# A streaming-encoder trunk on one Trainium2 core: the down projection's passes begin and end with plain quads, the PSUM banks swap roles, and the last half has three mixed groups

## The chip, the core and the metric

The kernel runs on one NeuronCore of a Trainium2 chip. The core has five engines that run side by side, each with a queue of its own: TensorE (PE) does matrix products into PSUM, VectorE (DVE), ScalarE (ACT) and GpSimd (POOL) do element work, and SyncE (SP) issues most transfers. The time is the device time of one launch in microseconds (us), the median of several runs.

## The reference

The input is `x`, 256 tokens of width 2048 in float32. Two layers follow, and each has a token mixer (a convolution module in layer 0, latent attention in layer 1) and then a squared-ReLU MLP:

```python
def sq_relu_mlp(h, w1, w2):
    return jnp.square(jax.nn.relu(h @ w1)) @ w2

for layer in range(DEPTH):                       # DEPTH = 2
    h = rms_norm(x, norm_mixer_g[layer])
    x = x + (conv_module if layer % 2 == 0 else mla)(h, ...)
    h = rms_norm(x, norm_mlp_g[layer])
    x = x + sq_relu_mlp(h, mlp_w1[layer], mlp_w2[layer])
return rms_norm(x, final_norm_g)
```

`w1` is 2048x8192 and `w2` is 8192x2048. The change lies in the product with `w2`, the down projection.

## The kernel before

**Precision.** Every float32 operand is split in two parts that TensorE takes at full speed: `hi` is a rounded copy (made on ACT, lines 169 and 487) and `lo` is the rest (raw minus `hi`, made on DVE, lines 173 and 488). `mm3` (lines 200 to 204) forms one product as three matmuls: hi*hi, lo*hi and hi*lo. The parts of the weights lie in two rings of `WB = 6` tiles, and the raw weights in a ring of three tiles that SP fills from HBM, 1 MB each. So the weights can be prepared only as far ahead as these rings are free.

**An MLP in halves.** `mlp(layer, ...)` goes through the 8192 hidden columns in two halves (`hf`). In each half the up projection computes eight groups `g` of 512 hidden columns (lines 619 to 660). Each group takes four of the eight PSUM banks in turn, and is then squared, scaled, split and kept in SBUF as `gs[g]`. Then the down projection (lines 661 to 707) multiplies these eight groups with 4096 rows of `w2`. I write a half as (layer, hf), from (0,0) to (1,1).

**Passes and quads.** The down projection goes over the 2048 output columns in two passes of 1024 (`n` = 0 and `n` = 2). One step is a *quad*: 256 rows of `w2` by 1024 columns, for all 256 tokens.
- A *plain* quad (`Sums.plain`, line 548) makes the four output blocks (2 halves of the tokens by 2 column blocks) straight, with 8 products, which are 24 matmuls. Each block adds up in a bank of its own, the four *e* banks.
- A *mixed* quad (`Sums.mixed`, line 535) uses a seven-product scheme in the manner of Strassen and Winograd: 7 products, 21 matmuls. It needs sums and differences of the weight blocks (`mixed_weights`, lines 480 to 500: three subtractions and four lower parts on DVE, against two lower parts for a plain quad) and of the activations (`mixed_inputs`). Three products go to the e banks, four to the *u* banks.

`MIXED` says which groups are mixed in each half: groups 0, 2, 4 and 6 in three halves, and 0, 2 and 4 in (0,1). Each group gives two quads.

**The end of a pass.** When the last mixed quad is done, `Sums.join` (line 565) turns the four u banks into the missing parts of the four blocks: a copy on ACT and four additions on DVE, into four SBUF tiles *a, b, c, d* (`room()`, a ring of four). POOL sends each tile to the residual stream `xs` with an accumulating transfer of 256 KB (`put`, line 563), in the order a, c, d, b. I call these the puts. When the last plain quad is done, `Sums.close` (line 577) adds two e banks to `xs` on DVE (line 583) and sends the other two with a copy on ACT (line 586) and two more puts.

**The order of a pass.** Lines 672 to 684 spread the mixed quads among the plain ones. Before, a pass begins with mixed quads, as many as line 677 gives for the first plain quad (two where four groups are mixed, one where three are); the last mixed quad stands ahead of the third last plain quad (`TAIL = 3`), and `join` ahead of the last but one. `Sums.__init__` (line 524) takes eight banks, the first four as u and the last four as e, in every pass.

**The second pass of a second half.** For `last` halves the pass `n = 2` is done by `product_A` (line 404) with the plain groups, one column block after the other, and the hook `between` (line 691) puts the mixed quads among those of the first block. Its index `u` is -1 ahead of the first plain group. In (1,1) it is followed at once by the final norm: `before` (line 1829) multiplies finished parts of `xs` with the final gain on DVE (`gained`, line 1787), the squares for the norm are made on ACT (line 400), and line 377 adds an e bank to `xs`.

**What sets the order.** The tile framework orders the instructions of each engine when the kernel is built; on the chip each engine goes through its own list in that order, and waits at an instruction until its semaphores are there.

Of the kernel before, what the change touches and what calls it, by code (L numbers as in the profile page):

```python
# [21 lines left out]
T = 2  # L22
# [18 lines left out]
PAD_O = 56  # L41
WB = 6
LOOK = WB // 2 - 1
MIXED = {(0, 0): (0, 2, 4, 6), (0, 1): (0, 2, 4), (1, 0): (0, 2, 4, 6), (1, 1): (0, 2, 4, 6)}
N_MIXED = 4
TAIL = 3


SIDE = {KC - 3: 2, KC - 2: 4}
# [29 lines left out]
def trunk_kernel(  # L79
# [59 lines left out]
    def nm(s):  # L139
        uid[0] += 1  # L140
        return f"{s}_{uid[0]}"


    def acc_tile():
        return psum["acc"].tile([P, NB], F32, tag="acc", name=nm("acc"))
# [45 lines left out]
    def load_split(srcs, nj):  # L191
        return split(load(srcs, nj), nc.vector)

    def rows(w, k0, nk, c0, n):

        return w[k0 * P : (k0 + nk) * P, c0 : c0 + n].rearrange(
            "(j p) n -> p j n", p=P
        )
# [106 lines left out]
    at, cols = 0, []  # L305
# [31 lines left out]
    def step(n=1000):  # L337
        while steps and n > 0:
            n -= 1
            steps.pop(0)()  # L340
# [180 lines left out]
    class Sums:  # L521


        def __init__(self, n):
            self.n = n
            self.u = [acc_tile() for _ in range(4)]
            self.e = [[acc_tile() for _ in range(2)] for _ in range(T)]
            self.begun = set()

        def first(self, ps):  # L530
# [58 lines left out]
    def mlp(layer, ssq, next_gain, finish=None, before=None, beside=None, after_up=None):  # L589

        with ExitStack() as cx:
# [7 lines left out]
            def v_tile():  # L599
                return mp.tile([P, 2, S], F32, tag="v", name=nm("v"), bufs=4)  # L600
# [4 lines left out]
            def scales():  # L605
                r = rms_rstd(ssq[:, :, :NNB], NNB, D, "n")
                r2 = small.tile([P, T], F32, tag="r2", name=nm("r2"))
                nc.vector.tensor_tensor(r2, r, r, op=ALU.mult)
                o = acc_tile()
                for t in range(T):  # L610
                    nc.tensor.transpose(o[:, t * P : (t + 1) * P], r2[:, t : t + 1].broadcast_to([P, P]), ident)
                nc.scalar.activation(r2_row, o[:, :S], AF.Copy)

            for hf in range(HALVES):
                last = hf == HALVES - 1
                mixed = MIXED[layer, hf]
                plain = [g for g in range(ng) if g not in mixed]
                gs = {}
                for g in range(ng):
                    ps = [acc_tile() for _ in range(4)]  # L620
                    c0 = (hf * nkh + 4 * g) * P
                    for u in range(KC // 4):
                        if u == KC // 4 - 1:
                            step()
                        wj = load_split([rows(mlp_w1[layer], 4 * u, 4, c0, NB)], 4)
                        for j in range(4):
                            k = 4 * u + j
                            wh, wl = wj(j)
                            for b in range(4):
                                bs = slice(b * P, (b + 1) * P)  # L630

                                nc.tensor.matmul(ps[b], wh[:, bs], xhl(k), start=k == 0, stop=False)  # L632
                                nc.tensor.matmul(ps[b][:, :S], wl[:, bs], xh(k), start=False, stop=k == KC - 1)  # L633
                        step(6)
                    if hf == g == 0:
                        scales()
                    if beside is not None and g == 2:
                        beside(mp)
                        beside = None
                    if g in mixed or g in plain[len(plain) + len(mixed) - N_MIXED :]:  # L640
                        shape = [P, 2, 7, P] if g in mixed else [P, 4, S]
                        gs[g] = [mp.tile(shape, F32R, tag=f"s{c}", name=nm(f"s{c}"), bufs=N_MIXED) for c in "hl"]
                    else:
                        gs[g] = [mp.tile([P, 4, S], F32R, tag=f"g{c}", name=nm(f"g{c}"), bufs=ng - N_MIXED) for c in "hl"]
                    gh, gl = gs[g]
                    for b2 in range(2):
                        v = v_tile()
                        for b in range(2):
                            o = ps[2 * b2 + b]
                            nc.scalar.activation(v[:, b, :], o[:, S:], AF.Copy)  # L650
                            nc.vector.tensor_tensor(v[:, b, :], o[:, :S], v[:, b, :], op=ALU.add)
                        nc.vector.scalar_tensor_tensor(out=v, in0=v, scalar=0.0, in1=v, op0=ALU.max, op1=ALU.mult)
                        row = r2_row.rearrange("p (a n) -> p a n", a=1).broadcast_to([P, 2, S])
                        nc.vector.tensor_tensor(v, v, row, op=ALU.mult)
                        if g in mixed:
                            mixed_inputs(v, gh[:, b2], gl[:, b2])
                            continue
                        bs = slice(2 * b2, 2 * b2 + 2)
                        nc.scalar.activation(gh[:, bs, :], v, AF.Copy)
                        nc.vector.tensor_tensor(gl[:, bs, :], v, gh[:, bs, :].bitcast(F32), op=ALU.subtract)  # L660
                nssq, add, prepare = residual_stage(last, next_gain)
                w, k_lo = mlp_w2[layer], hf * nkh
                at_kt = lambda i: lambda k, t: gs[k // 4][i][:, k % 4, t * P : (t + 1) * P]
                hi, lo = at_kt(0), at_kt(1)
                ms = [(g, b) for g in mixed for b in range(2)]
                due = []

                def mixed_quad(sums, i):
                    g, b = ms[i]
                    sums.mixed(w, k_lo + 4 * g + 2 * b, gs[g][0][:, b], gs[g][1][:, b], i == len(ms) - 1)  # L670

                for n in range(0, NNB - 2 * last, 2):
                    sums = Sums(n)
                    ks = [4 * g + 2 * b for g in plain for b in range(2)]
                    at = 0
                    for i, k in enumerate(ks):
                        upto = -(-len(ms) * (i + 1) // (len(ks) - TAIL + 1))
                        while at < min(upto, len(ms)):
                            mixed_quad(sums, at)
                            at += 1  # L680
                        if i == len(ks) - 2:
                            sums.join(room)
                        sums.plain(w, k_lo + k, hi, lo, k, i == len(ks) - 1)
                    sums.close(room)
                    if last:
                        due += [n, n + 1]
                if last:
                    sums = Sums(NNB - 2)
                    n2 = NNB - 2

                    def between(n, u, due):
                        if n == n2 and u < len(plain) - 1:
                            lo_i, hi_i = (len(ms) * i // len(plain) for i in (u + 1, u + 2))
                            for i in range(lo_i, hi_i):
                                mixed_quad(sums, i)
                        if n == n2 and u == len(plain) - 1:
                            sums.join(room)

                    if after_up is not None:
                        after_up()  # L700
                    product_A(
                        w, k_lo, nkh, hi, lo, add, prepare, range(n2, NNB), due,
                        finish=(lambda t: finish(nssq, t)) if finish is not None else None,
                        before=lambda: before(nssq),
                        groups=plain, banks={n2 + c: [sums.e[t][c] for t in range(T)] for c in range(2)},
                        begun=sums.begun, beside=between,
                    )
# [3 lines left out]
    with ExitStack() as cx:  # L711
# [235 lines left out]
        with tc.manual_schedule():  # L947
# [149 lines left out]
            for c in range(1, KC + 1):  # L1097
                n = UC * c
# [121 lines left out]
            for m in range(NP):  # L1220
# [25 lines left out]
                for q in {NP - 3: (0, 1, 4), NP - 2: (5, 2, 3), NP - 1: (6, 7)}.get(m, ()):  # L1246
                    t, i = divmod(q, NNB)
# [13 lines left out]
    def rotary_tables(pool):  # L1261
# [54 lines left out]
        nc.scalar.activation(cos, an2, AF.Sin)  # L1316

    ssq = mlp(0, ssq, g_mix[1], beside=rotary_tables)
    repool("a", acc=6, tr=2)


    with ExitStack() as cx:
        at = cx.enter_context(tc.tile_pool(name="at", bufs=1, reuse_waits="tile"))
# [320 lines left out]
        with tc.manual_schedule():  # L1644
# [8 lines left out]
            ps = [[acc_tile() for _ in range(2)] for _ in range(T)]  # L1653
            for k in range(KC):
                u, j = divmod(k, 2)
# [14 lines left out]
            ps = [acc_tile() for _ in range(T)]  # L1670
            for k in range(KC):
                u, j = divmod(k, 4)
# [59 lines left out]
            for g in range(NG):  # L1732
                for i in range(HG):
                    h = g * HG + i

                    n = -(-len(work) // (HG - i))
# [129 lines left out]
```

## Time and profile before

| what | value |
|---|---|
| median of 3 runs | 1953.53 us (1952.42 to 1954.0) |
| profiled execution | 1954.63 us, span 1952.8 us |
| PE, DVE, ACT, POOL busy | 1926.6, 1574.7, 1090.9, 259.2 us |
| mean granted clock of TensorE | 0.998 |

The page gives the busy time of each engine, and groups of instructions by line. `L488 DVE TENSOR_TENSOR lo<-raw,hi` is the DVE instruction of line 488 that writes `lo` from `raw` and `hi`; `x240` is the number of them. The idle time of a group is that of its engine just ahead of these instructions, and the name behind the arrow is what ended most of it. In a table by windows each engine has its busy time in that stretch and, in brackets, the number of its instructions there. A matmul's duration in the trace overlaps with the next one's, so a matmul's price is taken from the length of a stretch without waits, divided by the number of matmuls in it.

The eight down passes stand at 478 to 643 us (0,0), 821 to 990 us (0,1), 1427 to 1592 us (1,0) and 1769 to 1945 us (1,1).

### The profile page before, as it was taken

How to read it: one execution, taken by the hardware profiler on the slowest of the kernel's cores; microseconds unless marked ns; L12 is line 12 of the kernel's file. 1: busy time of each engine (PE TensorE's matmuls, PEld its weight loads, DVE VectorE, ACT ScalarE, POOL GpSimd, SP SyncE). 2: the span in 40 equal slices, each digit the busy share in tenths (PEclk: the TensorE clock that was granted, in tenths of full speed). 3: DMA queues.
4: the chain of work that ended last, by engine and by line, in shares of the span. 5: the costliest groups of instructions: out<-in, count | busy, mean ns of one | idle time of the engine just before them, and what ended most of it. 6: DMA issues, size and time to landing. Idle time of an engine off the chain costs nothing.

```text
span 1952.8 us, 28589 instructions
## 1 busy us (share of the span) xinstructions
PE 1926.6 (99%) x10811; PEld 1683.5 (86%) x10811; DVE 1574.7 (81%) x2436; ACT 1090.9 (56%) x1628; POOL 259.2 (13%) x216
## 2 busy tenths in 40 slices
PE   8999999999999999999999999999999999999997
PEld 8999888888888888888899998888888888888876
DVE  7999988877999677788866665877799967779996
ACT  5667755554555455455556655555555645555554
POOL 6999100000010000001002210000000010000000
PEclk9999999999999999999999999999999999999999
DMA  7765556654686766557764445566547686655755
GB/s 231 209 192 176 168 180 213 193 186 140 217 245 225 238 186 187 168 200 242 218 196 139 129 151 176 190 196 193 177 169 236 206 269 194 186 182 194 233 180 157
DMA packets 222057, 379.15 MB, mean 194 GB/s; under 512 B 16216, under 2 KB 91232, under 8 KB 221664
## 3 DMA queue, kind: packets, MB, share of 16 engines
q1 hardware_dynamic: 214256, 363.28, 58.0%
q0 software_dynamic: 6336, 11.54, 3.3%
q10 hardware_dynamic: 1328, 2.52, 0.4%
q8 instruction: 84, 1.38, 0.3%
q14 instruction: 53, 0.43, 0.1%
HBM read 363.68 MB, written 2.10 MB: 187 GB/s over the span
## 4 chain that ended last, share of the span: by engine, by line
PE 66%; issue 25%; DVE 4%; DMA 3%; ACT 1%; POOL 1%; SPq 0%; DVEq 0%; ACTq 0%; POOLq 0%
PE acc L632 18%; PE acc L633 9%; PE acc L202 9%; PE acc L204 9%; PE acc L203 8%; PE acc L776 8%; PE acc L1239 2%; DMA xs<-v 2%; DVE sum L863 1%; DVE lo L173 1%; POOL xs L563 1%; DVE lo L488 0%; DMA xs<-in_x 0%; ACT hi L169 0%; PE acc L1623 0%
## 5 line engine op out<-in xcount | busy, mean ns | idle before, releaser
L173 DVE TENSOR_TENSOR lo<-raw,hi 128x1024 fp32r<-128x1024 f32 (+2 forms) x511 | 607.7, 1204 | 262.1 <-ACT hi L169 256.7
L169 ACT ACTIVATE hi<-raw 128x1024 fp32r<-128x1024 f32 (+2 forms) x576 | 587.5, 1039 | 371.8 <-PE acc L632 208.5
L632 PE MATMUL acc<-xt,hi 128*128 128x512 f32 x2048 | 710.5, 390 | 0.0
L633 PE MATMUL acc<-xt,lo 128*128 128x256 f32 x2048 | 577.5, 282 | 0.0
L632 PEld LDWEIGHTS acc<-xt,hi 128*128 128x128 f32 x2048 | 384.3, 188 | 80.6
L633 PEld LDWEIGHTS acc<-xt,lo 128*128 128x128 f32 x2048 | 387.1, 189 | 0.2
L487 ACT ACTIVATE hi<-raw 128x1024 fp32r<-128x1024 f32 x240 | 222.5, 948 | 221.7 <-DVE raw L495 123.6
L488 DVE TENSOR_TENSOR lo<-raw,hi 128x1024 fp32r<-128x1024 f32 x240 | 256.1, 1087 | 33.3 <-ACT hi L487 29.3
L563 POOL DMA_DIRECT2D xs<-v x44 | 38.6, 942 | 1502.8 <-DVE lo L173 693.4
L202 PE MATMUL acc<-hi,sh 128*128 128x512 f32 x516 | 202.3, 392 | 5.6 <-ACT hi L487 5.4
L204 PE MATMUL acc<-lo,gh 128*128 128x512 f32 (+1 forms) x516 | 199.7, 388 | 3.2 <-DVE lo L173 3.2
L204 PE MATMUL acc<-lo,sh 128*128 128x512 f32 x516 | 199.5, 390 | 1.7 <-DVE lo L488 1.6
L202 PE MATMUL acc<-hi,gh 128*128 128x512 f32 (+1 forms) x516 | 200.3, 388 | 0.0
L203 PE MATMUL acc<-hi,gl 128*128 128x512 f32 (+1 forms) x516 | 200.0, 388 | 0.0
L776 PE MATMUL acc<-xt,hi 128*128 128x256 f32 x1024 | 180.2, 281 | 0.3 <-ACT b L1058 0.2
L203 PE MATMUL acc<-hi,sl 128*128 128x512 f32 x452 | 176.0, 389 | 0.0
L863 DVE SCALAR_TENSOR_TENSOR sum<-ub,w_dw,sum 128x256 f32<-128x256 f32 x409 | 164.3, 482 | 3.6 <-ACT sum L833 3.0
L173 POOL TENSOR_TENSOR lo<-raw,hi 128x1024 fp32r<-128x1024 f32 x65 | 154.9, 2406 | 17.3 <-ACT hi L169 17.3
L776 PEld LDWEIGHTS acc<-xt,hi 128*128 128x128 f32 x1024 | 154.7, 188 | 1.1 <-ACT xt L1042 0.6
L776 PE MATMUL acc<-xt,lo 128*128 128x256 f32 x512 | 139.2, 279 | 0.0
L202 PEld LDWEIGHTS acc<-hi,sh 128*128 128x128 f32 x516 | 96.9, 188 | 30.2 <-ACT hi L487 10.7
L204 PEld LDWEIGHTS acc<-lo,gh 128*128 128x128 f32 x516 | 96.9, 188 | 23.8 <-DVE lo L173 4.1
(306 smaller groups left out, 2543.6 us busy)
## 6 DMA issues: line engine op xcount, KB each, us to landing
raw<-in_mlp_w SPq DMA_DIRECT2D x256, 1024.0 KB, 5.4
raw<-in_conv_w_pw SPq DMA_DIRECT2D x62, 512.0 KB, 5.1
raw<-in_conv_w_pw SPq DMA_DIRECT2D x16, 1024.0 KB, 5.0
raw<-in_mla_w_o SPq DMA_DIRECT2D x16, 1024.0 KB, 5.4
xs<-v POOLq DMA_DIRECT2D x44, 256.0 KB, 7.2
raw<-in_mla_w_kv_up SPq DMA_DIRECT2D x8, 1024.0 KB, 5.4
raw<-in_mla_w_in SPq DMA_DIRECT2D x8, 576.0 KB, 3.8
raw<-in_mla_w_in SPq DMA_DIRECT2D x4, 1024.0 KB
```

Source lines behind the costliest of these rows:

```text
L169: nc.scalar.activation(hi, raw[:, js, :], AF.Copy)
L173: eng.tensor_tensor(lo, raw, hi.bitcast(F32), op=ALU.subtract)
L202: nc.tensor.matmul(ps, sh, mh, start=start, stop=False)
L203: nc.tensor.matmul(ps, sl, mh, start=False, stop=False)
L204: nc.tensor.matmul(ps, sh, ml, start=False, stop=stop)
L487: nc.scalar.activation(hi, src, AF.Copy)
L488: nc.vector.tensor_tensor(lo, src, hi.bitcast(F32), op=ALU.subtract)
L563: nc.gpsimd.dma_start(self.place(t, c), o, accum_op=ALU.add)
L632: nc.tensor.matmul(ps[b], wh[:, bs], xhl(k), start=k == 0, stop=False)
L633: nc.tensor.matmul(ps[b][:, :S], wl[:, bs], xh(k), start=False, stop=k == KC - 1)
L776: nc.tensor.matmul(pss[c][b][:, :S], w[i][:, bs], (xh, xl)[j](k), start=k == i + j == 0, stop=end and k == k0 + nk - 1 and (i, j) == terms ...
L863: nc.vector.scalar_tensor_tensor(out=out, in0=ubs[c][:, w : w + S], scalar=tap(c, w), in1=base, op0=ALU.mult, op1=ALU.add)
```

## The change

- `MIXED[1, 1]` loses group 6: the last half has three mixed groups, and five plain ones.
- Ahead of the first mixed quad of a pass there are now `HEAD` plain quads, two in the pass `n = 0` and one in the pass `n = 2`. `TAIL` goes from 3 to 2: the last mixed quad stands ahead of the last but one plain quad where four groups are mixed, and `join` directly ahead of the last one. (Where three groups are mixed, line 677's rounding up puts the last mixed quad ahead of the third last plain quad.)
- In the pass `n = 2` of a second half, no mixed quad stands ahead of the first plain group; they are spread over the gaps behind the plain groups.
- The banks: in the pass `n = 0` the first four of the eight banks are now the e banks, and the last four the u banks; in the pass `n = 2` it is the other way round. So the e banks of the second pass are the u banks of the first.

```diff
-MIXED = {(0, 0): (0, 2, 4, 6), (0, 1): (0, 2, 4), (1, 0): (0, 2, 4, 6), (1, 1): (0, 2, 4, 6)}
+MIXED = {(0, 0): (0, 2, 4, 6), (0, 1): (0, 2, 4), (1, 0): (0, 2, 4, 6), (1, 1): (0, 2, 4)}
-TAIL = 3
+HEAD, TAIL = (2, 1), 2
...
             self.n = n
-            self.u = [acc_tile() for _ in range(4)]
-            self.e = [[acc_tile() for _ in range(2)] for _ in range(T)]
+            ps = [acc_tile() for _ in range(8)]
+            e, self.u = (ps[:4], ps[4:])[:: 1 if n == 0 else -1]
+            self.e = [e[2 * t : 2 * t + 2] for t in range(T)]
...
-                    at = 0
+                    at, head = 0, HEAD[n // 2]
                     for i, k in enumerate(ks):
-                        upto = -(-len(ms) * (i + 1) // (len(ks) - TAIL + 1))
+                        upto = -(-len(ms) * (i - head + 1) // (len(ks) - head - TAIL + 1))
                         while at < min(upto, len(ms)):
                             mixed_quad(sums, at)
                             at += 1
-                        if i == len(ks) - 2:
+                        if i == len(ks) - TAIL + 1:
                             sums.join(room)
                         sums.plain(w, k_lo + k, hi, lo, k, i == len(ks) - 1)
...
                         if n == n2 and u < len(plain) - 1:
-                            lo_i, hi_i = (len(ms) * i // len(plain) for i in (u + 1, u + 2))
-                            for i in range(lo_i, hi_i):
+                            for i in range(*(len(ms) * max(i, 0) // (len(plain) - 1) for i in (u, u + 1))):
                                 mixed_quad(sums, i)
```

## The prediction

> **What bounds the kernel now.** I read the page first, for the busy engine, then the list of waits of TensorE (PE), then a table by windows over the down passes, and last the timelines of VectorE (DVE), ScalarE (ACT) and GpSimd (POOL) around the places where PE stood.
>
> ```profile
> span 1952.8 us, 28589 instructions
> PE 1926.6 (99%) x10811; PEld 1683.5 (86%) x10811; DVE 1574.7 (81%) x2436; ACT 1090.9 (56%) x1628; POOL 259.2 (13%) x216
> PEclk9999999999999999999999999999999999999999
> ```
>
> ```profile
> PE acc L202 <- ACT hi L487: 5.4, 7, 1.3
> PE acc L204 <- DVE lo L173: 3.2, 2, 2.3
> PE acc L204 <- DVE lo L488: 1.6, 3, 0.8
> ```
>
> PE is busy in 99% of the span at full clock, so the time can only move by matmuls added or removed and by PE's waits. The three rows are the largest of these waits but for one at the very start, and all three are waits for weight parts. Lines 487 and 488 are the mixed quads', line 173 the plain quads'. Columns below: window, its length, then busy time and count by engine.
>
> ```profile
> core 0: us, PE busy (x) PEld busy (x) DVE busy (x) ACT busy (x) POOL busy (x), PEclk, DMA share, GB/s
> 820.60:964.70 144.10, 144.10 (x638) 119.38 (x637) 122.42 (x130) 81.86 (x97) 8.90 (x12) 1.00 0.68 215
> 477.90:492.00 14.10, 12.99 (x55) 9.71 (x54) 12.91 (x19) 7.87 (x11) 0.00 (x0) 1.00 0.21 69
> 1426.40:1440.00 13.60, 12.49 (x53) 9.29 (x52) 12.41 (x19) 7.93 (x12) 0.00 (x0) 1.00 0.19 61
> 1769.20:1785.00 15.80, 14.51 (x63) 11.29 (x62) 14.62 (x21) 7.88 (x11) 0.00 (x0) 1.00 0.47 164
> 1785.00:1858.00 73.00, 73.00 (x324) 60.44 (x322) 67.90 (x72) 41.66 (x49) 5.26 (x6) 1.00 0.76 236
> 1858.00:1870.00 12.00, 8.82 (x35) 6.07 (x34) 9.34 (x11) 6.71 (x10) 0.00 (x0) 1.00 0.36 97
> 1870.00:1914.00 44.00, 43.35 (x186) 34.32 (x185) 43.18 (x46) 26.75 (x30) 0.86 (x1) 1.00 0.62 199
> 1914.00:1932.00 18.00, 14.80 (x64) 11.56 (x64) 12.89 (x19) 8.53 (x12) 2.64 (x3) 1.00 0.79 218
> ```
>
> The first row is half (0,1), with three mixed groups: PE never stands, and a matmul costs 144.10 / 638 = 0.226 us. What a window has beyond its count times 0.226 is lost: 1.67, 1.62 and 1.56 us at the starts of (0,0), (1,0) and (1,1); nothing in 1785 to 1858; then in (1,1) 4.09 at the start of its second pass, 1.96 in its middle and 3.54 near its end. That is 14.4 us, all in halves with four mixed groups.
>
> **The change, part by part.**
>
> *More matmuls.* Group 6 of (1,1) becomes plain: two quads in each of two passes take 24 matmuls instead of 21, so 12 more, 12 x 0.226 = **2.7 us**, on the path since PE is the bound. [...]
>
> *DVE's pace.* Timeline of DVE in the middle of (1,1), where it is the slower engine:
>
> ```profile
> 1867.71 1.82 DVE L488 TENSOR_TENSOR lo<-raw,hi 128x1024 fp32r<-128x1024 f32 x2
> ...
> 1881.22 2.35 DVE L173 TENSOR_TENSOR lo<-raw,hi 128x1024 fp32r<-128x1024 f32 x2
> 1883.49 1.22 DVE L488 TENSOR_TENSOR lo<-raw,hi 128x1024 fp32r<-128x1024 f32 x1
> ```
>
> Two mixed quads (M) take 1881.22 - 1867.71 = 13.51, so 6.76 us each; a plain one (P) 2.27. On PE M is 21 x 0.226 = 4.75 and P 5.42. So M M P costs DVE 15.8 against PE's 14.9: it falls back 0.9. M P gives it 1.1 back. (1,1) repeats M M P in its second pass and loses; with six mixed quads among five plain ones it has more P, as (0,1) has.
>
> *Starts of the halves (4.85 us lost).* One row of PE, then DVE:
>
> ```profile
> 477.97 0.39 PE L202 MATMUL acc<-hi,sh 128*128 128x512 f32 x1
> ...
> 479.18 0.42 DVE L651 TENSOR_TENSOR v<-acc,v 128x256 f32<-128x256 f32 x1
> ...
> 483.66 0.68 DVE L660 TENSOR_TENSOR gl<-v,gh 128x512 fp32r<-128x512 f32 x1
> ...
> 484.95 1.22 DVE L488 TENSOR_TENSOR lo<-raw,hi 128x1024 fp32r<-128x1024 f32 x1
> ...
> 487.96 1.23 DVE L488 TENSOR_TENSOR lo<-raw,hi 128x1024 fp32r<-128x1024 f32 x1 [1.18 <-ACT hi L487]
> ```
>
> The down pass begins at 477.97 with M M, while DVE still empties the last up group (until 484.3) between the parts of the second M, which are ready at 489.2, 11.2 us after the start. In the changed kernel's order the same interleaving holds the first M, behind P P. PE gets to it at 10.8 and to its last parts at 10.8 + 15 x 0.226 = 14.2: 3 us to spare. The next M is ready at 11.2 + 6.8 = 18.0, needed at 19.0. (0,0) and (1,0) then go P, M M P, M P, M M P, M P, P: by the paces above the last parts come 0.1 us early in the second M M, 1.3, 0.4 and so on. So it just fits: 0 kept, with 1 us each as the other end; I take 0.2 each, **0.4**. In (1,1) single M alternate with P, 0.
>
> *Bank roles.* The first P writes the banks of the last but one up group, long empty; the last group's are read until 479.6 (row 479.18) and are first written 10.8 us after the start. Cost 0; without that cover 1.6 us a half. In the second pass the first P writes what join has read; join is three DVE additions after b, some 3 us, and 10.8 us of PE work or more stand before that P. Cost 0; if DVE came to join 7 us late, each us more would be one of PE.
>
> *Second pass of (1,1) (4.09 + 1.96 lost).* DVE, ACT and POOL:
>
> ```profile
> 1855.99 1.22 DVE L495 TENSOR_TENSOR raw<-raw 128x1024 f32<-128x1024 f32 x1
> 1860.08 0.69 DVE L1787 TENSOR_TENSOR xs<-xs,gf 128x512 f32<-128x512 f32 x1 [2.87 <-ACT scratch L400]
> ...
> 1859.32 0.63 ACT L400 ACTIVATE scratch<-xs 128x512 f32<-128x512 f32 x1 [4.10 <-DMA xs<-v]
> ...
> 1854.52 1.76 POOL L563 DMA_DIRECT2D xs<-v  x2 [9.04 <-ACT hi L487]
> ```
>
> The put of 1854.52 lands for ACT's square at 1859.32; the gain behind it (line 1787) holds DVE for 2.87 us in the middle of the second M, whose parts PE wants. The order of the changed kernel has the whole first M ahead of that gain, and only the second plain group P1 behind it; ahead of P1, PE has P and M, 10.2 us. The pass ended (first start, 360 matmuls, 1.6 us lost) near 1852.4, so the square starts 6.9 us after the end; then 0.8 square, 1.0 `hi`, 0.7 gain and 1.2 `lo` make 10.6 us: at most 0.4 late for P1, and M M behind it falls back 0.9. I keep **0.5**; bounds 0 and 4.09. The middle goes to 0 by the pace.
>
> *Near the end (3.54 lost).* DVE, PE and the chain of waits:
>
> ```profile
> 1916.78 0.68 DVE L571 TENSOR_TENSOR v<-acc,v 128x512 f32<-128x512 f32 x1
> ...
> 1925.51 0.69 DVE L377 TENSOR_TENSOR xs<-acc,xs 128x512 f32<-128x512 f32 x1 [5.11 <-DMA xs<-v]
> 1926.11 1.21 DVE L173 TENSOR_TENSOR lo<-raw,hi 128x1024 fp32r<-128x1024 f32 x1
> ...
> 1927.38 0.50 PE L204 MATMUL acc<-lo,gh 128*128 128x512 f32 x1 [2.28 <-DVE lo L173]
> ...
> 1917.87 7.54 DMA xs<-v
> ```
>
> The addition of line 377 waits for put c, and the lower parts of the next group stand behind it. That wait stays. But DVE now reaches join when the last M ends, not late: c is made 2.6 us after that (b 0.7, one `lo` 1.2, c 0.7), the put lands 0.3 + 7.5 later, and add and `lo` (1.9) bring the second half of that group at 12.3. The first half stands ahead of the wait in the new order. PE wants the second half after two P and a half, 13.5. So 1.2 us to spare; a put of 9.9 (below) would be 1.2 late. I keep **0.3**, bounds 0 and 3.54.
>
> *Ends of the other passes.* In (0,0) and (1,0) join is one plain quad nearer to the end of the pass, in the other two not. From the chain:
>
> ```profile
> 1489.68 6.34 DMA raw<-in_mlp_w
> ...
> 1502.01 9.94 DMA xs<-v
> ...
> 1844.32 9.57 DMA xs<-v
> ```
>
> ACT's second copy in close needs the tile of the last put (a ring of four), which takes 9.6 to 9.9 us. With join 10.8 us before the end and DVE held by a weight load of 6.3 us, that put is issued about 4 us before the end and lands 6 after it. The first M's last parts then come 2.9 us later (copy, `hi`, `lo`), at 8.9, and are wanted at 5.42 + 3.39 = 8.8: 0, bound 2 us each. Its cover is the leading P.
>
> Sum: 14.4 - 0.4 - 0.5 - 0.3 - 2.7 = **10.5 us** less. The profiled execution took 1954.63, which gives 1944.1; it stands 1.1 above the median of the runs, 1953.53, from which I forecast **1943.0**.
>
> **The rivals.**
>
> *The blocked queues only move on.* Puts still hold DVE and ACT at both places of (1,1); if the puts are later than in these rows, the 4.09 and the 3.54 stay: 14.4 - 7.6 - 0.4 - 2.7 = 3.7 less, 1949.8. For it: both waits are still in the order. Against: the rows give 10 us of PE work ahead of the first and 1.2 to spare at the second. [...]
>
> *DVE falls behind in the denser passes.* P P M M P M M P has no slack: if no lead builds up, each M M P loses 0.9; three in the first and two in the second passes of (0,0) and (1,0) make ten, 9 us, and 10.9 - 9 = 1.9 less: 1951.6. Against: M P pairs stand between.
>
> *Slower.* The last put of join lands so late in (0,0) and (1,0) that the following M stand. It would be slower by 0.2% (3.9 us, about what a measurement tells from no change) from 14.4 us of new waits, 7.2 at each of the two, so a landing 13 us after the pass's end, 17 after issue, against 9.94 seen. At 7.5 each: 1943.0 + 15 = 1958.
>
> **How the numbers follow.** The forecast has 0.81, the moved queues 0.10, the denser passes 0.05, the slower one 0.04. The second and third gain 0.1 to 0.2%, so they count mostly as no change: faster 0.83, within 0.2% 0.12, slower 0.05. Range: everything regained gives 1953.5 - 11.7 = 1941.8, less the 1.1 that the runs spread below their median, some 1940.5; at the other end the moved queues, 1949.8.
>
> **What would show it.** Right: PE's waits for lines 487, 488 and 173 in the down passes fall from 10.2 us to under 2; (1,1) takes some 167 us instead of 175; DVE still waits for put landings, but PE not with it. Wrong: new rows of PE waiting for `hi` or `lo` some 20 to 35 us into (0,0) and (1,0); PE standing behind line 377 or line 1787 again; or lost time right behind the ends of the first passes.

## The result and the profile after

The changed kernel takes 1955.85 us (median of 20 runs, 1951.78 to 1960.31), beside 1952.47 us for the kernel before in the same session (20 runs, 1950.62 to 1955.23). The ratio is 1.0017, with a 95% interval of 1.0010 to 1.0023: slower by 0.17%, where 1943.0 had been forecast. The runs also spread more, over 8.5 us instead of 4.6. The spans of the two profiled executions, 1952.8 and 1954.8 us, differ by 2.0 us, the medians by 3.4. So the two traces can be used to find 2.0 us of the loss.

The page of the kernel after, its span and the row of the engines:

```profile
span 1954.8 us, 28567 instructions
PE 1929.8 (99%) x10823; PEld 1688.8 (86%) x10823; DVE 1557.0 (80%) x2404; ACT 1084.2 (55%) x1616; POOL 259.2 (13%) x216
```

There are twelve more matmuls, as announced, and 18 us less work on DVE. The waits of PE in the kernel after (what it waited for, us in total, times, longest):

```profile
PE acc L204 <- DVE lo L488: 3.9, 8, 0.6
PE acc L202 <- DVE xt L215: 2.0, 1, 2.0
PE acc L204 <- DVE lo L173: 2.0, 3, 0.9
...
PE acc L202 <- ACT hi L487: 1.2, 2, 0.6
PE acc L202 <- ACT hi L169: 0.6, 1, 0.6
```

The three waits of before, 10.2 us, have become 7.7 us of waits of the same kinds, in many small pieces, and a new one of 2.0 us on line 215. Where they stand, the table by windows tells. First three windows of the kernel before that the prediction did not show (columns as there: window, length, then busy time and count of PE, PEld, DVE, ACT, POOL, then clock, DMA share and GB/s):

```profile
477.90:643.20 165.30, 164.19 (x723) 134.91 (x721) 151.78 (x162) 92.72 (x104) 8.87 (x10) 1.00 0.70 220
1426.40:1591.80 165.40, 164.29 (x723) 135.02 (x722) 151.92 (x162) 93.38 (x106) 8.95 (x11) 1.00 0.70 224
1769.20:1944.90 175.70, 167.38 (x734) 134.71 (x732) 154.66 (x180) 94.53 (x118) 8.76 (x10) 1.00 0.63 198
```

The same halves in the kernel after, then (0,1) whole, and four stretches in which PE stands:

```profile
477.90:641.20 163.30, 163.30 (x723) 135.31 (x722) 153.47 (x165) 93.02 (x105) 8.86 (x10) 1.00 0.68 215
1432.40:1595.70 163.30, 163.30 (x723) 135.28 (x722) 153.20 (x165) 92.81 (x105) 8.74 (x10) 1.00 0.68 215
1773.20:1946.70 173.50, 168.87 (x746) 137.34 (x744) 141.00 (x163) 88.80 (x110) 8.75 (x10) 1.00 0.63 194
818.60:968.60 150.00, 146.72 (x638) 118.85 (x637) 124.06 (x133) 80.36 (x95) 8.93 (x12) 1.00 0.64 198
901.60:931.00 29.40, 26.61 (x109) 19.71 (x109) 18.43 (x19) 14.34 (x19) 1.75 (x2) 1.00 0.46 127
994.50:999.00 4.50, 2.53 (x20) 2.33 (x19) 2.72 (x11) 3.10 (x10) 0.00 (x0) 1.00 0.46 131
1868.00:1886.00 18.00, 14.74 (x57) 9.90 (x56) 15.47 (x17) 10.42 (x13) 0.00 (x0) 1.00 0.37 117
1924.00:1930.00 6.00, 5.10 (x22) 3.88 (x22) 4.04 (x9) 2.46 (x6) 0.00 (x0) 1.00 0.81 158
```

Read against 0.226 us for each matmul:
- (0,0) and (1,0) take 2.0 and 2.1 us less with the same 723 matmuls, and PE is busy in all of the window. This part came as forecast.
- (0,1) took 144.10 us for 638 matmuls before; now 150.00: **5.9 us more**. 29.40 - 109 x 0.226 = 4.8 of them lie at the start of its second pass.
- (1,1) takes 2.2 us less, where the terms of the prediction make 7.6 (11.15 of stalls, less 0.8 kept, less 2.7 of matmuls). Its second pass still loses 18.00 - 57 x 0.226 = 5.1 us at its start, and 1.0 near its end.
- Attention begins with a stand of PE of **2.0 us** (4.50 - 2.53).

The sum -2.0 - 2.1 - 2.2 + 5.9 + 2.0 = +1.6 is close to the 2.0 by which the spans differ.

What PE waits for at the start of the second pass of (0,1) is seen on POOL and ACT. The timeline of the two engines in the kernel after (start, length, engine, line, what; in brackets how long the engine was idle, and for what):

```profile
904.33 1.75 POOL L564 DMA_DIRECT2D xs<-v  x2 [9.34 <-ACT hi L487]
...
908.38 0.63 ACT L400 ACTIVATE scratch<-xs 128x512 f32<-128x512 f32 x1 [4.52 <-DMA xs<-v]
...
909.01 1.04 ACT L169 ACTIVATE hi<-raw 128x1024 fp32r<-128x1024 f32 x1
913.15 0.63 ACT L400 ACTIVATE scratch<-xs 128x512 f32<-128x512 f32 x1 [3.10 <-DMA xs<-v]
...
913.78 1.04 ACT L169 ACTIVATE hi<-raw 128x1024 fp32r<-128x1024 f32 x1
```

The two puts of `close` go out at 904.33 and 904.9. ACT's squares of that column block (line 400) wait for them, 4.52 and 3.10 us, and right behind each square in ACT's list stands an upper part `hi` of the next plain group's weights. DVE makes the lower part only from the upper one, so the weights of P1, and of the two mixed quads behind it, come late and PE stops in small steps from 914 to 931. The view of the put's line, for the put that `join` sends last and for the two of `close`, says how long they took (number, duration of the issue in ns and times of the issues; then how long ACT waited for them, and how often; then the time from issue to landing):

```profile
L564 POOL DMA_DIRECT2D xs<-v x2: 859/1006/1153, 893.2 to 893.8; - x2
...
DMA to landing us min/median/max: 5.8/7.8/9.9
```

```profile
L564 POOL DMA_DIRECT2D xs<-v x2: 862/1004/1147, 904.3 to 904.9; - x2
...
  ACT scratch L400: 7.6, 2
...
DMA to landing us min/median/max: 4.0/6.1/8.1
```

The last put of `join` (893.8, b) lands 9.9 us later, at 903.7; it adds to the same block of `xs` as the first put of `close`, which goes out right behind it, at 904.33. The second put of `close` then takes 8.1 us. In (1,1) the same view gives 4.0 and 8.1 us, and 7.6 us of ACT. In the kernel before, (0,1) had this view, on that kernel's line number, 563:

```profile
L563 POOL DMA_DIRECT2D xs<-v x2: 859/860/862, 903.6 to 905.0; - x2
...
  ACT scratch L400: 0.4, 1
...
DMA to landing us min/median/max: 3.4/3.4/3.5
```

So the theory to test was: *late puts*. The two puts of `close` land late, ACT's squares block the queue ahead of weight parts, PE runs out of weights. Its rival was *dense order*: not the puts, but the two mixed quads that now stand together near the start of the second pass let DVE fall behind. A third item, the stand at attention, had its own theory, a PSUM bank.

### The profile page after: what moved, and what is told of

Read it like the earlier page. It is cut to its first block, busy times and chain, and to the rows that moved or that the text cites. A ratio compares the mean times of both kernels' runs of the same rounds, so it can differ in the third digit from the quotient of the medians.

```text
span 1954.8 us, 28567 instructions
## 1 busy us (share of the span) xinstructions
PE 1929.8 (99%) x10823; PEld 1688.8 (86%) x10823; DVE 1557.0 (80%) x2404; ACT 1084.2 (55%) x1616; POOL 259.2 (13%) x216
## 4 chain that ended last, share of the span: by engine, by line
issue 25%; PE 19%; DVE 2%; DMA 2%; ACT 1%; POOL 1%; DVEq 0%; ACTq 0%; POOLq 0%
PE acc L633 6%; PE acc L634 3%; PE acc L204 3%; PE acc L202 3%; PE acc L203 3%; DMA xs<-v 2%; DVE lo L488 1%; POOL xs L564 1%; DVE lo L173 1%; DVE raw L495 0%; DMA raw<-in_mlp_w 0%; PE acc L1623 0%; ACT hi L487 0%; ACT hi L169 0%; PE tr L1614 0%
## 5 line engine op out<-in xcount | busy, mean ns | idle before, releaser
L173 DVE TENSOR_TENSOR lo<-raw,hi 128x1024 fp32r<-128x1024 f32 (+2 forms) x519 | 618.9, 1206 | 282.7 <-ACT hi L169 275.6
L487 ACT ACTIVATE hi<-raw 128x1024 fp32r<-128x1024 f32 x224 | 206.6, 948 | 201.0 <-DVE raw L495 118.4
L488 DVE TENSOR_TENSOR lo<-raw,hi 128x1024 fp32r<-128x1024 f32 x224 | 239.0, 1088 | 27.5 <-ACT hi L487 23.3
L204 PE MATMUL acc<-lo,sh 128*128 128x512 f32 (+1 forms) x524 | 204.4, 390 | 3.9 <-DVE lo L488 3.9
L202 PE MATMUL acc<-hi,sh 128*128 128x512 f32 (+1 forms) x524 | 203.9, 389 | 1.3 <-ACT hi L487 1.2
L204 PE MATMUL acc<-lo,gh 128*128 128x512 f32 x512 | 199.8, 390 | 2.0 <-DVE lo L173 2.0
L202 PE MATMUL acc<-hi,gh 128*128 128x512 f32 x512 | 199.9, 391 | 0.7 <-ACT hi L169 0.6
L203 PE MATMUL acc<-hi,gl 128*128 128x512 f32 x512 | 199.5, 390 | 0.0
L203 PE MATMUL acc<-hi,sl 128*128 128x512 f32 (+1 forms) x460 | 178.4, 388 | 0.0
L204 PEld LDWEIGHTS acc<-lo,sh 128*128 128x128 f32 x524 | 98.4, 188 | 27.8 <-DVE lo L488 8.0
```

Of the source, the lines that this page charges most:

```text
L173: eng.tensor_tensor(lo, raw, hi.bitcast(F32), op=ALU.subtract)
L202: nc.tensor.matmul(ps, sh, mh, start=start, stop=False)
L203: nc.tensor.matmul(ps, sl, mh, start=False, stop=False)
L204: nc.tensor.matmul(ps, sh, ml, start=False, stop=stop)
L487: nc.scalar.activation(hi, src, AF.Copy)
L488: nc.vector.tensor_tensor(lo, src, hi.bitcast(F32), op=ALU.subtract)
```

## The experiments

All ratios are to the kernel before, with 95% intervals; the kernel before had medians of 1952.73, 1952.22 and 1952.43 us in the three sessions.

**1. The old order of the second passes** (`second_old`). The mixed quads lead again, all else is as changed.

```diff
-                            for i in range(*(len(ms) * max(i, 0) // (len(plain) - 1) for i in (u, u + 1))):
+                            for i in range(*(len(ms) * i // len(plain) for i in (u + 1, u + 2))):
```

> The changed kernel with one line put back: the mixed quads of a last half's second pass stand between its plain groups as before (M P M P M P M P M M P instead of P M P M M P M P M M P). Late-put theory (the second put of close lands 11.5 us behind the end of the pass, and ACT's squares wait for it in front of weight parts): the put is as late, so the stalls at the start of the second passes of (0,1) and (1,1) (5.8 and 5.3 us) stay within 1.5 us: 1954 to 1957. Dense-order theory (leading plain group and two mixed quads side by side): the 5.8 us in (0,1) and some 4 of the 5.3 in (1,1) go: about 1946. By both, the wait at the start of attention stays, as the last two transposed tiles now lie in banks 1 and 0 and attention's first accumulator in bank 0: 2.1 to 2.5 us there.

1945.99 us, ratio 0.9966 (0.9954 to 0.9978). The view of the put's line in (0,1), the puts of `close`, and the two down passes of the second halves by windows:

```profile
  ACT scratch L400: 0.6, 2
...
DMA to landing us min/median/max: 3.3/3.3/3.3
```

```profile
1769.70:1936.30 166.60, 166.33 (x746) 137.99 (x744) 140.59 (x163) 88.74 (x110) 8.76 (x10) 1.00 0.64 202
818.70:962.70 144.00, 144.00 (x638) 119.31 (x637) 124.18 (x133) 81.98 (x97) 8.90 (x12) 1.00 0.66 208
```

Both second passes lose nothing that counts. By the time alone the dense-order theory has won, and the late-put theory's number is wrong. But its premise was not met either: the puts are no longer late. With the old order they land in 3.3 us instead of 4.0 and 8.1, though the order that was put back lies behind them. The order of the second pass acts on the puts, so this run could not separate the two. At attention the wait was 2.8 us, somewhat more than expected (see experiment 8).

**2. `join` one plain quad earlier** (`early`).

```diff
-                        if i == len(ks) - TAIL + 1:
+                        if i == len(ks) - TAIL + 1 - last:
```

> The changed kernel with join one plain quad further ahead of the end of the first passes in (0,1) and (1,1), as far as it stood before; all else as changed. Late-put theory: the last put of join lands before the pass ends, close's second put takes 3 to 4 us instead of 8, the stalls of 5.8 and 5.3 us at the start of the second passes fall under 1.5 each: 1945 to 1949. Dense-order theory: both stalls stay, 1954 to 1957.

1955.34 us, ratio 1.0019 (1.0007 to 1.0031), ten runs from 1949.91 to 1961.90. The edit did nothing: the framework gave every engine the same list of instructions as in the changed kernel, with other numbers for the tiles. It is a repetition of the changed kernel, then, and as such it tells more than was meant. Its profiled execution happened to be a quick one, with a span of 1950.0 us. The puts of `close` in (0,1), then that half by a window:

```profile
  ACT scratch L400: 3.7, 2
...
DMA to landing us min/median/max: 3.2/4.4/5.6
```

```profile
818.90:965.10 146.20, 145.15 (x639) 119.21 (x638) 124.00 (x133) 80.35 (x95) 8.93 (x12) 1.00 0.64 203
```

The instructions are the same. The second put takes 5.6 us instead of 8.1, ACT is held 3.7 us instead of 7.6, and (0,1) takes 146.20 instead of 150.00, (1,1) 170.60 instead of 173.50. The landing of the puts varies from one execution to the next, and PE's loss goes with it. Whether an earlier `join` would help was not tried.

**3. No puts in `close`** (`direct`). In the last halves the second column is added by DVE too; the order stays as changed.

```diff
-        def close(self, room):
+        def close(self, room, direct=False):
...
-                    if c == 0:
+                    if c == 0 or direct:
...
-                    sums.close(room)
+                    sums.close(room, last)
```

> The changed kernel, but in the last halves close adds its second column with two additions of DVE (0.69 us each) instead of two copies of ACT and two puts by POOL. Late-put theory: ACT's squares then wait for DVE and for the puts of join alone, which land 2 us behind the end of the pass instead of 11.5; the stalls of 5.8 and 5.3 us fall under 1.5 each: 1945 to 1949. Dense-order theory: both stalls stay or grow by 1.4 of DVE work: 1954 to 1958.

1946.25 us, ratio 0.9969 (0.9957 to 0.9981). The first of ACT's two squares in (0,1), then the two halves by windows:

```profile
904.37 0.63 ACT L400 ACTIVATE scratch<-xs 128x512 f32<-128x512 f32 x1 [0.91 <-DVE xs L584]
```

```profile
818.60:962.90 144.30, 144.30 (x639) 119.51 (x638) 124.92 (x135) 80.66 (x94) 7.19 (x10) 1.00 0.64 203
1769.00:1936.30 167.30, 166.78 (x746) 137.90 (x744) 141.59 (x165) 88.22 (x108) 7.03 (x8) 1.00 0.62 198
```

With the dense order in place and the puts gone, (0,1) loses nothing and (1,1) about 1 us. This is the separating run: PE's loss needs the late puts, and the pair of mixed quads alone does not make it. The runs also lie close together again, 1945.11 to 1947.40.

**4. Other banks at the end of (0,1)** (`warm3`). The changed kernel, with three single transposes that nobody reads.

```diff
                 elif gain is not None:
+                    for _ in range(3 * (n == NNB - 1)):
+                        keep_warm(ident, 1)
                     for j in range(2):
                         to_T(xs, 4 * n + 2 * j, xh, xl, gain)
```

> The changed kernel with three groups of one 128-column transpose each (into PSUM tiles that nobody reads) ahead of the last two transposed tiles of (0,1), which shifts these from banks 2 and 4 to banks 7 and 1; attention's first four accumulators stay in banks 0, 5, 4 and 3. Bank theory: the wait of 2.1 us of PE at attention's third accumulator goes, for 0.3 us of transposes: 1954.0, the rest as changed. Rival (the accumulator waits because the lower parts of xt themselves are late): the wait stays, 1956.1.

1952.36 us, ratio 0.9997 (0.9989 to 1.0006). The start of attention in the changed kernel, on PE, and the same place here by a window:

```profile
997.68 0.37 PE L202 MATMUL acc<-hi,xt 128*128 128x288 f32 x1 [1.97 <-DVE xt L215]
```

```profile
994.00:1000.00 6.00, 5.76 (x44) 5.38 (x43) 4.55 (x13) 4.20 (x12) 0.00 (x0) 1.00 0.35 98
```

The stand is gone and the bank theory holds. The gain in time, 3.5 us, is larger than the 1.8 expected, but the kernels with a leading plain group and these puts scatter by 6.2 to 12.0 us, so the size is not to be read from the median.

**5. Which part of the new order makes the puts late** (`lead_only`, `pair_only`). With three mixed groups the second pass began M P M P M in the old order, and the change made it P M P M M. One kernel has the leading plain group without the pair, the other the pair without the leading plain group.

```diff
-                            for i in range(*(len(ms) * max(i, 0) // (len(plain) - 1) for i in (u, u + 1))):
+                            for i in range(*(0, 0, 1, 2, 4, 6)[u + 1 : u + 3]):   # lead_only
+                            for i in range(*(0, 1, 3, 4, 5, 6)[u + 1 : u + 3]):   # pair_only
```

> The changed kernel with another order in the second passes of the last halves: the plain group still leads, but no two mixed quads stand together near the start (P M P M P M M P M M P instead of P M P M M P M P M M P). If the leading plain group is what makes the puts of close land late, (0,1) still loses 4 to 6 us and (1,1) as much: 1953 to 1956. If it is the pair M M behind the second plain group, both lose under 1: 1946 to 1947. At attention the two last transposed tiles stay in banks 2 and 4, so that wait of 2.1 us stays.

> The other half of the same split: a mixed quad leads as before, but two stand together behind the first plain group (M P M M P M P M P M P). Leading-group theory: no stall in (0,1) and under 1 us in (1,1), 1945 to 1947, as with the old order. Pair theory: 3 us or more lost in each, 1951 to 1955. At attention the last two tiles are in banks 1 and 0, so its wait of 2.9 us and the slow stretch of 1.5 behind it stay.

`lead_only`: 1952.93 us, ratio 1.0005 (0.9996 to 1.0014), runs from 1950.87 to 1957.05. `pair_only`: 1947.61 us, ratio 0.9979 (0.9970 to 0.9988). The puts of `close` in (1,1) of the two kernels, then (1,1) by a window, `lead_only` first each time:

```profile
  ACT scratch L400: 9.4, 1
...
DMA to landing us min/median/max: 7.8/8.2/8.5
```

```profile
  ACT scratch L400: 1.4, 2
...
DMA to landing us min/median/max: 3.7/3.9/4.0
```

```profile
1769.10:1942.90 173.80, 169.06 (x746) 138.91 (x744) 140.78 (x163) 88.75 (x110) 8.75 (x10) 0.99 0.63 194
1770.10:1937.60 167.50, 166.80 (x746) 137.89 (x744) 140.82 (x163) 88.84 (x110) 8.73 (x10) 1.00 0.63 201
```

It is the leading plain group. With it the puts take up to 8.5 us and hold ACT 9.4 us; with a mixed quad ahead they take 4.0. (1,1) takes 173.80 us with the leading plain group, as in the changed kernel, and 167.50 with the pair alone. In (0,1) the profiled execution of `lead_only` lost only some 1.5 us, less than expected, with 4.3 us of ACT behind the puts, and its median lies just below the 1953 to 1956 of the leading-group theory. The pair alone costs 1.6 us against `second_old` by the medians, though its runs scatter by 6.1 us, and that is just above the 1945 to 1947 expected.

**6. The third group alone** (`only3`). The kernel before with group 6 of (1,1) made plain.

```diff
-(1, 1): (0, 2, 4, 6)}
+(1, 1): (0, 2, 4)}
```

> The kernel before, with group 6 of (1,1) made plain and nothing else. If the stalls of its second pass came from four mixed groups, 9.6 us go and 2.7 come, and the start of the half, now M P instead of M M, loses its 1.6 too: 1952.7 - 8.5 = 1944.2; nothing changes in the other halves, and the wait at the start of attention does not come. If the stalls came from the puts alone, they stay: 1953 to 1955.

1945.40 us, ratio 0.9964 (0.9952 to 0.9977), runs from 1945.12 to 1945.45. The half (1,1) by a window:

```profile
1769.10:1935.30 166.20, 166.20 (x746) 138.13 (x744) 139.18 (x160) 89.14 (x110) 8.75 (x10) 1.00 0.65 209
```

PE never stands in 166.20 us: the twelve extra matmuls bring the half down from 175.70. This one line is the best part of the change.

**7. The fourth group back** (`fourth`). The kernel of experiment 1, with `MIXED[1, 1]` as before.

```diff
-(1, 1): (0, 2, 4)}
+(1, 1): (0, 2, 4, 6)}
```

> The changed kernel with the old order of the second passes, and four mixed groups in (1,1) as before. Pace theory (with eight mixed quads among four plain groups DVE is the slower engine): 12 matmuls less, 2.7 us, but the stalls of the kernel before in its second pass (4.1, 2.0 and 3.5 us) come back in part: 1948 to 1953. Late-put theory alone: the fourth group costs nothing and saves 2.7: 1943.3.

1955.58 us, ratio 1.0017 (1.0008 to 1.0026). The longest wait of PE, and two windows behind the end of the first pass of (1,1):

```profile
PE acc L202 <- ACT hi L487: 5.3, 3, 4.8
```

```profile
1864.60:1871.20 6.60, 6.16 (x14) 4.04 (x15) 6.60 (x8) 5.00 (x8) 0.00 (x0) 0.50 0.13 24
1871.20:1877.80 6.60, 6.60 (x30) 5.49 (x29) 6.46 (x8) 3.05 (x4) 0.00 (x0) 0.99 0.81 293
```

Against 1945.99 the fourth group costs 9.6 us, more than the range expected. PE stands 4.8 us, and then runs at a granted clock of 0.50 for 6.6 us: 14 matmuls there, and 30 in the next stretch of the same length, at 0.99.

**8. The best of the parts** (`second_old_w`, `best`). Experiment 1 with the three transposes of experiment 4, and the same with the `close` of experiment 3.

> The kernel with the old order of the second passes, and three single transposes ahead of the last two transposed tiles of (0,1), which puts these into banks 3 and 7 instead of 1 and 0, so that attention's first three accumulators (banks 0, 5, 4) are free. Bank theory: PE's wait of 2.9 us at the first accumulator falls under 0.6, and the slow stretch behind it goes too (14 matmuls of 288 columns at 0.240 us instead of 0.133, 1.5 us): 1945.99 - 2.9 - 1.5 + 0.6 = about 1942. If the slow stretch has another cause, 1943.7. If the wait is for data and not for a bank, 1946.3.

> The kernel before this one, and close adds its second column with DVE instead of puts in the last halves. If the puts of close cost nothing any more once the second pass begins with a mixed quad, it takes the same time within 1 us, about 1942; if they still held ACT for part of the time, up to 1 us less; if 1.4 us more of DVE work a half now shows, 1 to 3 us more.

1942.33 us, ratio 0.9950 (0.9938 to 0.9962), and 1942.23 us, ratio 0.9950 (0.9937 to 0.9962). Both beat the kernel before by 10 us and the changed one by 13.5. PE's wait for line 215 in `second_old`, then in `second_old_w`; behind each, the stretch after it in the same kernel:

```profile
PE acc L202 <- DVE xt L215: 2.8, 1, 2.8
```

```profile
992.00:995.40 3.40, 3.40 (x15) 3.40 (x16) 0.18 (x2) 3.12 (x10) 0.00 (x0) 0.53 0.03 12
```

```profile
PE acc L202 <- DVE xt L215: 0.8, 1, 0.8
```

```profile
992.00:995.40 3.40, 3.40 (x28) 3.40 (x27) 0.22 (x3) 3.09 (x10) 0.00 (x0) 1.00 0.06 24
```

The wait fell from 2.8 to 0.8 us (under 0.6 had been expected), and with it went the stretch at a clock of 0.53: 28 matmuls in 3.40 us at 1.00, instead of 15. That the two kernels take the same time says that the puts of `close` cost nothing once the second pass begins with a mixed quad. Both times are near the 1943.0 that the prediction gave to the change, but they come from the other order of the second pass.

## Why the prediction was wrong

- **More matmuls**: right, twelve.
- **Starts of the halves**: right, and a little better. The stalls of (0,0), (1,0) and (1,1) are gone (in (1,1) PE is busy in all of the first 15.80 us), and the passes P P M M P M never fall behind; of the 0.4 us kept nothing came. The windows give 2.0 and 2.1 us for the first two, not 1.5 and 1.4.
- **Denser passes, the second rival**: did not happen in the first halves, as PE is busy in all of 163.30 us.
- **Ends of the other passes, and the slower rival**: late puts were feared behind the first passes of (0,0) and (1,0), where nothing was lost. The slower outcome came by the same kind of transfer, but in the second halves, where the squares of the next norm wait for it.
- **Second pass of (1,1)**: this step failed. It took the landing from the old order: "The put of 1854.52 lands for ACT's square at 1859.32", 6.9 us after the pass's end. From it and one square it had P1's weights ready at 10.6 us, against 10.2 us of PE work. In the new order a `hi` of P1 stands behind each of the two squares. The second put landed 8.1 us after its issue instead of 5.4 at most, behind a last put of `join` that itself landed after the pass's end, and the second square started at 1868.12, 11.9 us after the end of the pass at 1856.2. Kept were 0.5 us; 5.1 stayed. The first rival, that the blocked queues only move on, was the right mechanism for this place; its chance of 0.10 was too low, and its price left out (0,1).
- **(0,1)**: the omission behind the largest part of the miss. The prediction used this half as its example of a pass that never stands, and never costed its new second pass, although the edit of `between` applies to it just as to (1,1). It lost 5.9 us. The slack there was small: before, ACT stood 0.4 us behind the puts.
- **Near the end of (1,1)**: mis-sized. 0.3 us was kept and 1.0 stayed: the addition of line 377 still waited 5.4 us for put c, and the lower part behind it came 0.9 us late for PE, where 1.2 us to spare had been counted. In all (1,1) lost 7.3 us (173.50 against the 166.20 of `only3`), about 1 us of it in the middle of the pass. Nearly all of it goes when the second pass begins with a mixed quad.
- **Bank roles: "Cost 0"**: wrong in its consequence. Cost 0 was right for the swap itself, as the lines that swap the roles do nothing. With them or without them, the kernel of experiment 1 is built into the same lists of instructions with the same bank for every tile. But with the new order of quads the last two transposed tiles of (0,1) came to lie in banks 2 and 4 instead of 7 and 6. Attention's third accumulator gets bank 4, and had to wait for DVE to read the tile there: 2.0 us, in a stage that the change does not touch.

In sum the forecast change of -10.5 us missed by 12.5 between the two traces: 5.9 in (0,1), 5.4 in (1,1) and 2.0 at attention, less 1.2 that the starts gave beyond their term (2.0 + 2.1 against 1.67 + 1.62 - 0.4); what is left, 0.4, is within the reading of the windows.

What stays open: why a leading plain group makes the puts late. With it, the last put of `join` in (0,1) took 9.9 us in the changed kernel and 8.9 in `lead_only`; with a mixed quad ahead, 6.8 in `second_old` and 5.8 in `pair_only`, though issued within 0.8 us of the same moment. One thing beside it differs in the same way, the next weight load on SP. The changed kernel first, then `second_old`:

```profile
894.59 10.93 SPq L159 DMA_DIRECT2D raw<-in_mlp_w  x2
...
899.42 13.71 SPq L159 DMA_DIRECT2D raw<-in_mlp_w  x3
```

With the leading plain group SP issues the next 1 MB load 0.8 us behind that put (894.59 against 893.8; 0.7 in `early`), with a mixed quad ahead 5.2 us behind it (899.42 against 894.2). In the kernel before, which begins with a mixed quad, that put had a load 0.8 us behind it too and took 9.5 us, but it was issued at 890.7 and had landed before `close` sent anything. So the load right behind the put is the suspect. It isn't shown to be the cause: in (1,1) of the kernel before a put took 9.6 us with the next load 6.4 us away, and no run held the order fixed and moved the loads alone.

## What to carry to other kernels

When an edit sits in code that several stages share, cost it in every stage that runs it, above all in the stages that show no wait today: their slack is what is about to be spent. A transfer's landing time read from the old order isn't a constant of the new one (the puts of `close` in (0,1): 3.5 us before, up to 8.1 after). Where an engine's list has a consumer of that transfer directly ahead of work that the busy engine needs, as ACT's squares stood 7.6 us here ahead of P1's `hi`, ask what the landing may grow to, or take the transfer off the path, as the two additions on DVE did. And after any reordering compare which PSUM bank each tile gets up to the next stage, since a moved bank made a stage wait here that nobody edited, 2.0 us at attention.

## What the runs showed of the hardware

Two things had not been expected. First, a short stand of PE cost more than its length. After 2.8 us of waiting at attention in `second_old`, and after 4.8 us in `fourth`, the granted clock was 0.53 and 0.50 for the next stretch, which cost some 1.5 us more in the one (14 matmuls at 0.240 instead of 0.133 us) and 3.4 in the other (6.60 - 14 x 0.226). In `early` a stand of only 2.0 us, the same as in the changed kernel, was followed by this window, while the changed kernel's clock stayed at 1.00:

```profile
995.00:998.00 3.00, 3.00 (x15) 3.00 (x14) 0.00 (x0) 2.98 (x9) 0.00 (x0) 0.51 0.00 0
```

The slow stretch lasted about 3.4 us in `second_old` and 6.6 in `fourth`; the next one of the same length had a clock of 1.00 and 0.99. The lower clock came behind a stand of 2.8 us in `second_old`, and behind one of 2.0 us in `early` (0.51) and `direct` (0.66 from 991 to 995), but not behind the 2.0 us of the changed kernel. What decides whether it comes is not shown.

Second, the puts. One and the same list of instructions had the second put of `close` land after 8.1 us in one execution and after 5.6 in another. All kernels whose second pass begins with a plain group and has these puts scatter, the changed one over 8.5 us, `early` over 12.0, `warm3` over 6.7 and `lead_only` over 6.2; with a leading mixed quad and single spacing, `only3` scatters over 0.3 and `second_old` over 2.1, and with the puts taken out, `direct` over 2.3. These last three had five runs each, the others ten or more, so part of their quiet may be the smaller number. The leading group isn't the only source, since `pair_only` scatters over 6.1, `fourth` over 3.4 and the kernel before over 4.6.
